# Turning the memory's keys by crossbar DMA instead of TensorE transposes

## The chip, the cores and the metric

One NeuronCore of a Trainium2 chip runs the kernel. The metric is the device time of one execution in microseconds. Inside the core, TensorE (PE, with its weight loads shown apart as PEld), VectorE (DVE), ScalarE (ACT) and GpSimd (POOL) each work through their own instructions in the order in which they were issued; SyncE (SP) issues most of the transfers. The engines wait for each other by semaphores.

## The reference

One transformer layer on 256 tokens of width 1024, in float32. What matters here is the part called cross-attention, and the piece ahead of it.

```python
def _cross_attention(h, m, w_xq, w_xkv, xq_norm_g, xk_norm_g, w_xo):
    q = (h @ w_xq).reshape(B, S, XATTN_HEADS, XATTN_HEAD_DIM)      # 4 heads of 256
    kv = (m @ w_xkv).reshape(B, M, 2, XATTN_HEADS, XATTN_HEAD_DIM) # 256 memory rows
    k, v = kv[:, :, 0], kv[:, :, 1]
    q = _rms_norm(q, xq_norm_g)
    k = _rms_norm(k, xk_norm_g)
    s = jnp.einsum('bshd,bmhd->bhsm', q, k, preferred_element_type=jnp.float32) * (XATTN_HEAD_DIM ** -0.5)
    p = jax.nn.softmax(s, axis=-1).astype(v.dtype)
    o = jnp.einsum('bhsm,bmhd->bshd', p, v).reshape(B, S, D_MODEL)
    return o @ w_xo

# in reference():
        x = x + jnp.concatenate([pool, attn], axis=-1) @ w_out[l]
        h = _rms_norm(x, norm_xattn_g[l])
        m = _rms_norm(mem, norm_mem_g[l])
        x = x + _cross_attention(h, m, w_xq[l], w_xkv[l], xq_norm_g[l], xk_norm_g[l], w_xo[l])
```

`pool` is a mixer of running means, `attn` a self-attention with 8 heads of 64. A feed-forward block with a short convolution follows.

## The kernel before, in words

**Numbers.** A float32 product is made from parts: every operand is written as a high part (fp32r, by a cast on ACT, `part_h`, L273 and L275) and a low part (the rest, by a subtraction on DVE, `part_l`, L279 and L281), and two or three PE passes add up. Weights arrive as `raw` chunks of 1 MB (two units each, a ring of three chunks), are cast to `wh` on ACT (L214) and subtracted to `wl` on DVE (L225). `need(u)` casts some units ahead of the one that PE uses; the load of a chunk can leave once the chunk that held its place in the ring has been subtracted.

**Stages, in PE's order.** The projections of the input (k, q, v, u); the memory's keys in two chunks of 512 columns, `a_chunk(18, ...)` for heads 0 and 1 and `a_chunk(22, ...)` for heads 2 and 3 (L418 to L423); between their matmuls lie the score transposes of the self-attention and the matmuls of the pool mixer; then `finish(job_attn, job_pool)`, in which the self-attention's outputs are multiplied (L651 to L655) and put into the tile `cat`; then w_out in eight output tiles (`resid_stage(26, cat, ...)`, L301 to L305), w_xq in eight, the values, w_xo, the feed-forward. `cat` has eight pieces: 0 to 3 from the pool mixer, 4 to 7 from the self-attention. Every output tile of w_out takes all eight, in the order of k.

**Order.** Work beside the matmuls is written as generators, called jobs. PE's loops call `tick()`: twice for each k of `a_chunk`, after every second k of an output tile and once more behind it (four in a tile); `finish()` ticks until its jobs are done. At a tick each live job, oldest first, goes on to its next `yield`. `yield from wait(n)` lets n ticks pass, with n from lists like `WAIT_KEY`. So the lists decide where an instruction stands in the order of its engine, and an instruction that is issued early and must wait holds up whatever its engine has behind it.

**The keys.** `key_job(c, bks)` starts when the matmuls of chunk c have been issued: `key_job(0)` just ahead of `a_chunk(22)`, `key_job(1)` just behind it. It squares the keys with a sum on ACT (L731), forms 1/rms (`head_scale`: three small DVE instructions, then twelve on POOL, L253 to L256, into `rs4y` for chunk 0 and `rs5y` for chunk 1), scales the keys out of PSUM into `kn` on DVE (L739, one half of the memory's rows at a time), turns them on PE into a bank of PSUM (L747, four 128 x 128 transposes for a head), and splits the bank into the tile `kx`.

**The cross-attention's scores.** `x_job(hp)` multiplies queries and keys of heads 2hp and 2hp+1 (L290 to L292). It is started behind query tiles 3 and 7 of w_xq, waits eight ticks, and then until the jobs named in its `after(...)` have ended.

The end of the kernel turns the residual with the crossbar already (`turn_job`, L1052 to L1060): a copy on ACT that sorts the 16-bit halves of the floats into two planes, a transposing DMA issued by SP, and copies on ACT that join the halves again.

Of the kernel before, what the change touches and what calls it, by code (L numbers as in the profile page):

```python
# [12 lines left out]
U16 = mybir.dt.uint16  # L13
# [4 lines left out]
P = 128  # L18
# [3 lines left out]
TT = S // P  # L22
# [5 lines left out]
XD = 256  # L28
# [21 lines left out]
WAIT_SCORE = [5, 4, 0, 9, 1, 6, 3, 1, 3, 5]  # L50
WAIT_ATTN = [0, 15, 1, 2, 2, 0, 0]
WAIT_POOL = [0, 8, 0, 7, 1, 5, 2, 2, 0]
WAIT_KEY = [0, 8, 7, 2, 0, 13, 5]
WAIT_R1 = [5]
WAIT_X = [3, 0, 0, 0, 10, 0, 6, 13, 8]
WAIT_VALUE = [32]
# [37 lines left out]
def block_kernel(ctx: ExitStack, tc: tile.TileContext, wpack: bass.AP, xpack: bass.AP, scal: bass.AP,  # L94
                 memT: bass.AP, table: bass.AP, out: bass.AP):
    nc = tc.nc
    pe, act, dve, pool = nc.tensor, nc.scalar, nc.vector, nc.gpsimd
# [11 lines left out]
    def bank():  # L109
        turn[0] += 1  # L110
        return psum.tile([P, 512], F32, name=f"bank{turn[0]}", tag="bank", bufs=8)

    def t2(name, dtype=F32):
        return temps.tile([P, 512], dtype, name=name, tag="t2", bufs=19)
# [4 lines left out]
    def pair(name, cols=KT * S):  # L119

        return pairs.tile([P, 2 * cols], F32R, name=name, tag="pair", bufs=4)

    def sm(name, n, dtype=F32):
        return small.tile([P, n], dtype, name=name)
# [4 lines left out]
    def go(gen):  # L129

        job = [gen, True]
        jobs.append(job)
        step(job)
        return job
# [16 lines left out]
    def wait(n):  # L151
        for _ in range(n):
            yield

    def after(*which):
        while any(job[1] for job in which):
            yield
# [5 lines left out]
    ident = tab[:, T_ID:T_ID + P]  # L163
# [95 lines left out]
    def head_scale(name, ss, n, width, small_eps):  # L259

        x = sm(name, TT * n)
        for tt in range(TT):
            c = slice(tt * n, (tt + 1) * n)
            dve.tensor_scalar(x[:, c], ss[:, c], 1.0 / width, col(small_eps, tt), op0=ALU.mult, op1=ALU.add)
        return rsqrt(x, TT * n)

    def part_h(h, src, scale=None):
        if scale is None:
            act.copy(h, src)  # L273
        else:
            act.activation(h, src, AF.Copy, scale=scale)  # L275

    def part_l(l, src, h, scale=None):
        if scale is None:
            dve.tensor_tensor(l, src, h.bitcast(F32), op=ALU.subtract)  # L279
        else:  # L280
            dve.scalar_tensor_tensor(l, src, scale, h.bitcast(F32), op0=ALU.mult, op1=ALU.subtract)  # L281
# [6 lines left out]
    def three(o, stat, mov, start, stop):  # L288

        pe.matmul(o, stat[0], mov[0], start=start, stop=False)  # L290
        pe.matmul(o, stat[0], mov[1], start=False, stop=False)  # L291
        pe.matmul(o, stat[1], mov[0], start=False, stop=stop)  # L292
# [14 lines left out]
    def col(t, c):  # L307
        return t[:, c:c + 1]

    def tiles(t, *dims):  # L310

        names = " ".join("abc"[:len(dims) - 1])
        sizes = dict(zip("abc", dims[:-1]))
        v = t.rearrange(f"p ({names} z s) -> p z {names} s", z=2, **sizes)
        return v[:, 0], v[:, 1], t.rearrange(f"p ({names} w) -> p {names} w", **sizes)
# [403 lines left out]
    kn = {}  # L719
# [3 lines left out]
    def key_job(c, bks):  # L723

        while "em" not in rows:
            yield
        yield from wait(WAIT_KEY[6])
        for mt in range(TT):
            kn[c, mt] = t2(f"kn{c}{mt}")
            for i in range(2):  # L730
                act.activation(kn[c, mt][:, i * XD:(i + 1) * XD], bks[mt][:, i * XD:(i + 1) * XD], AF.Square,  # L731
                               accum_out=col(ssk[c], 2 * mt + i))
        yield from wait(WAIT_KEY[0])
        y = head_scale(f"hm{c}", ssk[c], 2, XD, rows["em"])
        yield from wait(WAIT_KEY[1])
        for mt in range(TT):
            for i in range(2):
                r = slice(i * XD, (i + 1) * XD)
                dve.tensor_scalar(kn[c, mt][:, r], bks[mt][:, r], col(y, 2 * mt + i), None, op0=ALU.mult)  # L739
            yield from wait(WAIT_KEY[2])  # L740
        for i in range(2):
            h = 2 * c + i
            yield from wait(WAIT_KEY[3])
            b = bank()
            for dd in range(2):
                for mt in range(TT):
                    pe.transpose(b[:, (dd * 2 + mt) * P:(dd * 2 + mt + 1) * P],  # L747
                                 kn[c, mt][:, i * XD + dd * P:i * XD + (dd + 1) * P], ident)
            bb = b.rearrange("p (d s) -> p d s", d=2)
            yield from wait(WAIT_KEY[4])  # L750
            part_h(kxv[0][:, 2 * h:2 * h + 2], bb)
            yield from wait(WAIT_KEY[5])
            part_l(kxv[1][:, 2 * h:2 * h + 2], bb, kxv[0][:, 2 * h:2 * h + 2])

    for _ in range(MEM_TICKS):
# [4 lines left out]
    finish(job_k)  # L760
    kxv = tiles(pair("kx"), KT, S)
    job_key0 = go(key_job(0, bk0))
    bk1 = [bank(), bank()]
    look[0] = LOOKS[5]
    a_chunk(22, mgv, bk1)
    job_key = go(key_job(1, bk1))
    finish(job_attn, job_pool)

# [64 lines left out]
    job_r1 = []  # L833

    def x_job(hp):

        hs = (2 * hp, 2 * hp + 1)
        yield from after(job_key0, job_key, *job_r1)
        bs = [bank() for _ in range(TT)]
        for tt in range(TT):  # L840
            for i, h in enumerate(hs):
                o = bs[tt][:, i * XD:(i + 1) * XD]
                for dd in range(2):
                    q = [t[:, 2 * h + dd, tt * P:(tt + 1) * P] for t in xqv[:2]]
                    three(o, q, [t[:, 2 * h + dd] for t in kxv[:2]], dd == 0, dd == 1)
            if tt == 0:
                b = bank()
                b4 = b.rearrange("p (a s) -> p a s", a=2 * TT)
                for t in range(TT):
                    for i, h in enumerate(hs):  # L850
                        pe.transpose(b4[:, 2 * t + i], sqp[h][:, t * P:(t + 1) * P], ident)
            yield from wait(WAIT_X[0])
            if tt == 0:
                ssx = sm(f"ssx{hp}", 2 * TT)
                dve.tensor_reduce(ssx, b4, axis=AX.X, op=ALU.add)
                s2 = head_scale(f"hx{hp}", ssx, 2, XD, r1[0])
                pool.tensor_scalar(s2, s2, XD ** -0.5, None, op0=ALU.mult)
        pvs = []
        mx, nb, sums2, rec = (sm(f"{n}{hp}", 2 * TT) for n in ("xmx", "xnb", "xsum", "xrec"))
        for tt in range(TT):  # L860
            bb = bs[tt].rearrange("p (h k) -> p h k", h=2)
            c = slice(2 * tt, 2 * tt + 2)
            dve.tensor_reduce(mx[:, c], bb, axis=AX.X, op=ALU.max)
            dve.scalar_tensor_tensor(nb[:, c], mx[:, c], -1.0, s2[:, c], op0=ALU.mult, op1=ALU.mult)
            yield from wait(WAIT_X[1])
            pv = t2(f"xp{hp}{tt}").rearrange("p (h k) -> p h k", h=2)
            for j in range(2):
                cc = 2 * tt + j
                act.activation(pv[:, j], bb[:, j], AF.Exp, bias=col(nb, cc), scale=col(s2, cc),
                               accum_out=col(sums2, cc))  # L870
            pvs.append(pv)
        yield from wait(WAIT_X[2])
        for tt in range(TT):
            c = slice(2 * tt, 2 * tt + 2)
            dve.reciprocal(rec[:, c], sums2[:, c])
            for j in range(2):
                dve.tensor_scalar(pvs[tt][:, j], pvs[tt][:, j], col(rec, 2 * tt + j), None, op0=ALU.mult)
            yield from wait(WAIT_X[3])
        yield from wait(WAIT_X[4])
        if not ptv:  # L880
            ptv.extend(tiles(pair("xpt"), XH, TT, S))
        for j, h in enumerate(hs):
            b = bank()
            bb = b.rearrange("p (m q) -> p m q", m=TT)
            for mt in range(TT):
                for tt in range(TT):
                    pe.transpose(bb[:, mt, tt * P:(tt + 1) * P], pvs[tt][:, j, mt * P:(mt + 1) * P], ident)
            yield from wait(WAIT_X[5])
            part_h(ptv[0][:, h], bb)
            yield from wait(WAIT_X[6])  # L890
            part_l(ptv[1][:, h], bb, ptv[0][:, h])
        yield from wait(WAIT_X[7])
# [18 lines left out]
    for f in range(KT):  # L911
        b = bank()
# [32 lines left out]
    for h in range(XH):  # L945
        b = bank()
# [78 lines left out]
    for i in range(NFF):  # L1025
# [8 lines left out]
        for g in range(2):  # L1034
            b = bank()
# [41 lines left out]
    for c in range(2):  # L1077
        bk = [bank(), bank()]
        n = NFF - (BY_ROWS if c else 0)
# [18 lines left out]
    for tt in range(TT):  # L1098
        last = tt == TT - 1
        m = NFF - (BY_HALVES if last else 0)  # L1100
# [16 lines left out]
        b = bank()  # L1117
# [107 lines left out]
```

## Time and profile before

| | |
|---|---|
| median of 3 runs | 379.22 us (378.79 to 379.77) |
| the profiled execution | 379.3 us, span 377.3 us |
| PE | 372.6 us busy, 99% of the span |
| DVE | 314.3 us, 83% |
| ACT | 257.3 us, 68% |
| POOL | 69.5 us, 18% |

The span is the time from the first to the last instruction that the profile shows; the execution's time has 2.0 us more. Matmuls are pipelined and a PE instruction's shown duration overlaps the next ones, so what a group of them costs is read from the distance between starts. In a row of a timeline stand the start, the duration (both in us), the engine, the line of the program, the operation, the tile written and the tiles read, the shape, a count, and, in brackets, how long the engine stood idle before and what ended that.

### The profile page before, as it was taken

Reading aid. Unit: us, or ns where it says so; the run is one execution under the profiler, and the core shown is the slowest. Engines: PE = TensorE matmul, PEld = TensorE weight load, DVE = VectorE, ACT = ScalarE, POOL = GpSimd, SP = SyncE. Lnnn points to the kernel's source line nnn. Section 1 sums busy time; section 2 is a strip of 40 time slices with the busy share of each in tenths; the row PEclk is TensorE's granted clock in tenths of the full one; section 3 lists DMA queues with packets and bytes.
Section 4 is the critical chain, followed back from the end, with each engine's and each line's share of the span. In section 5 each row is a group of like instructions: output and inputs, shape, how many; then the busy total and the mean of one; then the engine's idle time right before and its main releaser. Section 6 shows DMA issues by size and latency. Waiting matters only on the chain.

```text
span 377.3 us, 5801 instructions
## 1 busy us (share of the span) xinstructions
PE 372.6 (99%) x2072; PEld 321.0 (85%) x2072; DVE 314.3 (83%) x561; ACT 257.3 (68%) x495; POOL 69.5 (18%) x151
## 2 busy tenths in 40 slices
PE   9999999999999999999999999999999999999996
PEld 7788888888888988898888888888888888888885
DVE  5699999979878969689979999999999999725611
ACT  5767887977567655855665588788777787993400
POOL 0253885143831132200320000000000000000000
PEclk9999999999999999999999999999999999999999
DMA  7996382454506535353536156655556635792501
GB/s 264 421 379 219 122 333 74 160 213 128 209 2 222 224 111 195 140 224 112 186 125 248 28 196 224 222 187 187 200 210 222 215 129 217 177 378 67 213 0 56
DMA packets 16203, 70.17 MB, mean 186 GB/s; under 512 B 5552, under 2 KB 6192, under 8 KB 8624
## 3 DMA queue, kind: packets, MB, share of 16 engines
q1 hardware_dynamic: 15888, 69.29, 51.1%
q10 hardware_dynamic: 288, 0.52, 0.4%
q8 instruction: 16, 0.26, 0.3%
q14 instruction: 11, 0.09, 0.1%
HBM read 67.71 MB, written 1.05 MB: 182 GB/s over the span
## 4 chain that ended last, share of the span: by engine, by line
PE 96%; DMA 2%; DVE 0%; ACT 0%; issue 0%; DVEq 0%
PE bank L305 33%; PE bank L304 17%; PE bank L418 7%; PE bank L423 7%; PE bank L420 7%; PE bank L1083 4%; PE bank L1088 4%; PE bank L1085 4%; DMA raw<-wpack 2%; PE bank L292 1%; PE bank L290 1%; PE bank L291 1%; PE bank L1105 1%; PE bank L1104 1%; PE bank L576 1%; PE bank L615 1%
## 5 line engine op out<-in xcount | busy, mean ns | idle before, releaser
L225 DVE TENSOR_TENSOR wl<-raw,wh 128x1024 fp32r<-128x1024 f32 (+1 forms) x127 | 150.7, 1202 | 10.5 <-ACT wh L214 10.3
L214 ACT CAST wh<-raw 128x1024 fp32r<-128x1024 f32 (+1 forms) x125 | 126.5, 1028 | 24.9 <-DMA raw<-wpack 22.6
L305 PE MATMUL bank<-hs,wh 128*128 128x512 f32 x304 | 105.4, 391 | 0.0
L304 PE MATMUL bank<-hs,wl 128*128 128x256 f32 x304 | 85.1, 280 | 0.0
L305 PEld LDWEIGHTS bank<-hs,wh 128*128 128x128 f32 x304 | 56.8, 187 | 12.5
L304 PEld LDWEIGHTS bank<-hs,wl 128*128 128x128 f32 x304 | 57.5, 189 | 0.0
L1002 ACT ACTIVATE y<-up,sc 128x256 f32<-128x256 f32 x44 | 26.2, 603 | 22.2 <-DVE up L989 17.7
L305 PE MATMUL bank<-h,wh 128*128 128x512 f32 x112 | 39.4, 394 | 0.0
L1009 DVE SCALAR_TENSOR_TENSOR y<-up,sc,y 128x255 f32<-128x255 f32 (+1 forms) x88 | 36.9, 488 | 0.0
L304 PE MATMUL bank<-h,wl 128*128 128x256 f32 x112 | 31.7, 283 | 0.0
L305 PEld LDWEIGHTS bank<-h,wh 128*128 128x128 f32 x112 | 21.0, 188 | 4.7
L1083 PE MATMUL bank<-wh,act 128*128 128x512 f32 x72 | 22.2, 389 | 0.0
L1085 PE MATMUL bank<-wh,act 128*128 128x512 f32 x72 | 22.2, 389 | 0.0
L1088 PE MATMUL bank<-wl,act 128*128 128x512 f32 x72 | 22.1, 389 | 0.0
L275 ACT ACTIVATE h<-sc 128x256 fp32r<-128x256 f32 x16 | 8.2, 511 | 20.3 <-DVE sc L793 20.2
L305 PE MATMUL bank<-cat,wh 128*128 128x512 f32 x62 | 21.8, 393 | 0.0
L305 PE MATMUL bank<-ox,wh 128*128 128x512 f32 x62 | 21.6, 394 | 0.0
L304 PEld LDWEIGHTS bank<-h,wl 128*128 128x128 f32 x112 | 21.2, 189 | 0.0
L418 PE MATMUL bank<-wh,xg 128*128 128x512 f32 x64 | 20.2, 397 | 0.5 <-ACT wh L214 0.4
L418 PE MATMUL bank<-wh,mg 128*128 128x512 f32 x64 | 20.7, 405 | 0.0
L801 POOL TENSOR_TENSOR h_acc<-h_sq,h_acc 128x256 f32<-128x256 f32 x14 | 12.9, 922 | 41.6 <-ACT h_sq L800 41.5
L423 PE MATMUL bank<-wl,mg 128*128 128x512 f32 x64 | 20.0, 394 | 0.0
(265 smaller groups left out, 733.1 us busy)
## 6 DMA issues: line engine op xcount, KB each, us to landing
raw<-wpack SPq DMA_DIRECT2D x59, 1024.0 KB, 4.9
raw<-wpack SPq DMA_DIRECT2D x4, 512.0 KB, 7.6
mraw<-memT SPq DMA_DIRECT2D x4, 256.0 KB, 8.5
sc<-xpack SPq DMA_DIRECT2D x3, 256.0 KB, 4.6
raw<-wpack ACTq DMA_DIRECT2D x2, 256.0 KB, 3.4
raw<-wpack SPq DMA_DIRECT2D x2, 256.0 KB, 4.1
out<-o SPq DMA_DIRECT2D x2, 256.0 KB, 2.6
tab<-table SPq DMA_DIRECT2D x1, 480.0 KB, 9.4
```

Source lines behind the costliest of these rows:

```text
L214: copy(split[u][0][:, r], unit(u)[:, r])
L225: dve.tensor_tensor(l[:, r], unit(u)[:, r], h[:, r].bitcast(F32), op=ALU.subtract)
L304: pe.matmul(b[:, 0:n], stat[1], mov[:, 0:n], start=start, stop=False, skip_group_check=not wide_first)
L305: pe.matmul(b, stat[0], mov, start=False, stop=stop, skip_group_check=not wide_first)
L418: pe.matmul(bk[tt], a[tt][0], wv[0], start=k == 0, stop=False)
L420: pe.matmul(bk[tt], a[tt][1], wv[0], start=False, stop=False)
L423: pe.matmul(bk[tt], a[tt][0], wv[1], start=False, stop=k == KT - 1)
L1002: act.activation(y[:, g * S:(g + 1) * S], src[:, g * S:(g + 1) * S], AF.Identity, bias=col(sc, C_CB + f), scale=col(sc, C_CW + 2 * 2 * NFF ...
L1009: dve.scalar_tensor_tensor(yy[:, j:], uu[:, :S - j], col(sc, C_CW + (2 - j) * 2 * NFF + f), yy[:, j:], op0=ALU.mult, op1=ALU.add)
L1083: pe.matmul(bk[tt], a[tt][0], w[0], start=k == 0, stop=False)
L1085: pe.matmul(bk[tt], a[tt][1], w[0], start=False, stop=False)
L1088: pe.matmul(bk[tt], a[tt][0], w[1], start=False, stop=k == NFF - 1)
```

## The change

The PE transposes of the keys go. Each half of the rows of a chunk, once scaled, is copied by ACT into two planes of 16-bit halves (`kp`), one SP queue transfer for each half transposes the planes into `kf`, and for each head ACT joins the halves into a float tile `kT` in SBUF, from which the high and low parts are made. The pauses of the key jobs are new: the squares come right after the chunk's matmuls, the scaling earlier, and chunk 1 lets 32 ticks pass between its transposes and its first join. The first cross-attention job waits for the first key job only.

```diff
-WAIT_KEY = [0, 8, 7, 2, 0, 13, 5]
+WAIT_KEY = [1, 8, 1, 0, 0, 2, 0]
+WAIT_FLAT = [[6, 1, 0, 16, 3, 6], [2, 2, 0, 32, 2, 6]]
...
         yield from wait(WAIT_KEY[0])
         y = head_scale(f"hm{c}", ssk[c], 2, XD, rows["em"])
         yield from wait(WAIT_KEY[1])
+        flat = []
         for mt in range(TT):
             for i in range(2):
                 r = slice(i * XD, (i + 1) * XD)
                 dve.tensor_scalar(kn[c, mt][:, r], bks[mt][:, r], col(y, 2 * mt + i), None, op0=ALU.mult)
-            yield from wait(WAIT_KEY[2])
+            yield from wait(WAIT_FLAT[c][mt])
+            planes = t2(f"kp{c}{mt}").bitcast(U16)
+            act.copy(planes.rearrange("p (z n) -> p z n", z=2),
+                     kn[c, mt].bitcast(U16).rearrange("p (n z) -> p z n", z=2))
+            flat.append((planes, t2(f"kf{c}{mt}").bitcast(U16)))
+            if mt == 0:
+                yield from wait(WAIT_KEY[2])
+        pauses = WAIT_FLAT[c]
+        yield from wait(pauses[2])
+        for planes, to in flat:
+            nc.sync.dma_start_transpose(to.rearrange("p (g s) -> p g s", g=8), planes)
+        yield from wait(pauses[3])
         for i in range(2):
             h = 2 * c + i
-            yield from wait(WAIT_KEY[3])
-            b = bank()
-            for dd in range(2):
-                for mt in range(TT):
-                    pe.transpose(b[:, (dd * 2 + mt) * P:(dd * 2 + mt + 1) * P],
-                                 kn[c, mt][:, i * XD + dd * P:i * XD + (dd + 1) * P], ident)
-            bb = b.rearrange("p (d s) -> p d s", d=2)
-            yield from wait(WAIT_KEY[4])
+            kT = t2(f"kT{c}{i}")
+            for mt in range(TT):
+                act.copy(kT.bitcast(U16).rearrange("p (d m s z) -> p m z d s", d=2, m=2, z=2)[:, mt],
+                         flat[mt][1].rearrange("p (z i d s) -> p i z d s", z=2, i=2, d=2)[:, i])
+                yield from wait(pauses[4])
+            bb = kT.rearrange("p (d s) -> p d s", d=2)
             part_h(kxv[0][:, 2 * h:2 * h + 2], bb)
-            yield from wait(WAIT_KEY[5])
+            yield from wait(pauses[5])
             part_l(kxv[1][:, 2 * h:2 * h + 2], bb, kxv[0][:, 2 * h:2 * h + 2])
...
-        yield from after(job_key0, job_key, *job_r1)
+        yield from after(*([job_key0] if hp == 0 else [job_key0, job_key]), *job_r1)
```

## The prediction

> **What bounds the kernel now.** I read the page's busy shares and its chain that ended last, then the timelines of PE, ACT, DVE and POOL between 69 and 106 us, where the memory's keys are made.
>
> ```profile
> PE 372.6 (99%) x2072; PEld 321.0 (85%) x2072; DVE 314.3 (83%) x561; ACT 257.3 (68%) x495; POOL 69.5 (18%) x151
> PE 96%; DMA 2%; DVE 0%; ACT 0%; issue 0%; DVEq 0%
> ```
>
> PE is busy 99% of the span, and 96% of the chain is PE. No later wait on weights stands in that chain, so a microsecond taken from PE's stream, or a hole put into it, should arrive at the end in full. ACT and DVE count only where they hold PE up.
>
> **What is removed.** Sixteen PE transposes, in four groups of four.
>
> ```profile
> L747 PE MATMUL bank<-tab,kn x16: 270/272/273, 92.5 to 115.7; 128*128 128x128 f32 x16
> ...
> 103.11 0.39 PE L305 MATMUL bank<-cat,wh 128*128 128x512 f32 x1
> 103.34 0.60 PE L747 MATMUL bank<-tab,kn 128*128 128x128 f32 x4
> ...
> 103.90 0.40 PE L305 MATMUL bank<-cat,wh 128*128 128x512 f32 x1
> ...
> 104.25 0.40 PE L305 MATMUL bank<-cat,wh 128*128 128x512 f32 x1
> ```
>
> L305 to L305 is 0.35 us without a group (103.90 to 104.25) and 0.79 with one (103.11 to 103.90): a group costs 0.44, four cost 1.77. That is the gain, 379.3 - 1.8 = 377.5 if nothing else moves. The Trainium skill (TensorE: Matmul & The Clock Gate, Part 4: PE-mode transpose) gives about 275 ns for a transpose inside a kernel; counted as PE time that would be an estimate of 4.4 us for sixteen, and the sum below would be 377.7. The trace has the same 272 ns as duration, but four overlap and take 0.44 us of the stream, so the measurement decides for 1.77.
>
> **What is added, and its prices.** The end of the kernel already turns another tensor this way.
>
> ```profile
> L1052 ACT COPY rp<-sc x4: 1030/1041/1042, 319.9 to 330.8; 128x1024 uint16<-128x1024 uint16 x4
> L1060 ACT COPY rT<-rf x8: 758/764/770, 327.8 to 342.3; 128x512 uint16<-128x512 uint16 x8
> L1056 SPq DMA_TRANSPOSE rf<-rp x4: 1237/1358/2888, 321.0 to 331.9; - x4
> DMA to landing us min/median/max: 3.1/6.1/7.4
> ```
>
> Four plane copies (4 x 1.04) and eight joins (8 x 0.76) are 10.3 us more for ACT. The casts and subtractions of the turned keys stay, from SBUF instead of PSUM; I count them as equal. SP gets four transposes of 1.2 to 2.9 us each, and they are queued between weight loads.
>
> **Where the steps fall.** A job goes on at every tick; I counted ticks from the second half of the keys' matmuls (16 ticks, two per k), tick 0 being its start. First chunk: its squares were at tick 5 and come to 0; scaling of the first half of the rows was at 13, comes to 9; its planes at 15; second half's scaling 20 to 16; its planes and both transposes at 17; joins at 33, 36, 45, 48; last subtraction at 57, as before. Second chunk: squares 21 to 16; planes 27 and 30, transposes 30; joins 62, 64, 72, 74; last subtraction 82 (was 73). The two cross-attention jobs start at 76 and 92, as before: with the relaxed condition the first does not wait for 82, and the second comes after it. So PE's order is unchanged but for the missing transposes.
>
> The trouble is at tick 20. There the attention's four outputs, cat tiles 4 to 7, are cast on ACT, and PE needs them at once, in the first output tile of w_out. Before, nothing of the keys stood ahead of them on ACT. Now the first planes (15), the second chunk's squares (16) and the second planes (17) do.
>
> ```profile
> 69.84 2.02 ACT L214 CAST wh<-raw 128x1024 fp32r<-128x1024 f32 x2
> 71.73 0.59 ACT L605 ACTIVATE p<-bank,nbs,sp 128x256 f32<-128x256 f32 x1
> ...
> 72.73 0.23 ACT L605 ACTIVATION_READ_ACCUMULATOR p<-bank,nbs,sp 128x1 f32 x1
> ...
> 75.37 0.43 ACT L731 ACTIVATE kn<-bank 128x256 f32<-128x256 f32 x1
> ...
> 76.81 0.44 ACT L624 COPY pt<-bank 128x256 f32<-128x256 f32 x1
> ...
> 81.44 0.47 ACT L275 ACTIVATE cat<-bank,sc 128x256 fp32r<-128x256 f32 x1 [0.55 <-DVE cat L281]
> ...
> 82.33 0.50 ACT L275 ACTIVATE cat<-bank,sc 128x256 fp32r<-128x256 f32 x1
> 84.24 0.47 ACT L275 ACTIVATE cat<-bank,sc 128x256 fp32r<-128x256 f32 x1 [1.42 <-DVE cat L281]
> 84.61 0.67 ACT L273 CAST cat<-bank 128x256 fp32r<-128x256 f32 x2
> ...
> 86.22 0.37 ACT L273 CAST cat<-bank 128x256 fp32r<-128x256 f32 x1 [0.28 <-PE bank L655]
> ```
>
> ```profile
> 73.81 0.16 DVE L607 RECIPROCAL recs<-sums 128x2 f32<-128x2 f32 x1
> ...
> 74.53 0.16 DVE L607 RECIPROCAL recs<-sums 128x2 f32<-128x2 f32 x1
> ...
> 77.28 0.17 DVE L246 TENSOR_SCALAR rs4y<-hm 128x4 int32<-128x4 int32 x1
> 77.36 0.69 DVE L701 TENSOR_TENSOR pooll<-pf,poolh 128x512 fp32r<-128x512 f32 x1
> 77.96 2.35 DVE L225 TENSOR_TENSOR wl<-raw,wh 128x1024 fp32r<-128x1024 f32 x2
> ...
> 82.94 0.88 DVE L739 TENSOR_SCALAR kn<-bank,rs4y 128x256 f32<-128x256 f32 x2 [0.51 <-POOL rs4y L256]
> 83.73 0.48 DVE L281 SCALAR_TENSOR_TENSOR cat<-bank,sc,cat 128x256 fp32r<-128x256 f32 x1
> ...
> 86.63 0.42 DVE L279 TENSOR_TENSOR cat<-bank,cat 128x256 fp32r<-128x256 f32 x1 [0.23 <-ACT cat L273]
> ```
>
> ```profile
> 77.53 0.57 POOL L253 TENSOR_TENSOR rs4t<-rs4y 128x4 f32<-128x4 f32 x1 [10.11 <-DVE rs4y L246]
> 78.18 1.06 POOL L254 TENSOR_TENSOR rs4t<-rs4t,hm 128x4 f32<-128x4 f32 x1
> 79.33 1.04 POOL L255 TENSOR_SCALAR rs4t<-rs4t 128x4 f32<-128x4 f32 x1
> ...
> 82.70 0.20 POOL L256 TENSOR_TENSOR rs4y<-rs4t,rs4y 128x4 f32<-128x4 f32 x1
> ```
>
> ```profile
> 87.61 0.28 PE L304 MATMUL bank<-cat,wl 128*128 128x256 f32 x1
> 87.73 0.40 PE L305 MATMUL bank<-cat,wh 128*128 128x512 f32 x1
> ...
> 88.79 0.40 PE L305 MATMUL bank<-cat,wh 128*128 128x512 f32 x1
> ```
>
> Before, the last cat tile was done on DVE at 87.05 (86.63 + 0.42), and PE's k=7 reads it at 88.79: a margin of 1.74 us. Now the same chain after the change.
>
> 1. The squares move ahead of the two weight casts at 69.84 and push what follows by 1.44 (75.37 to 76.81), so the softmax piece of 71.73 runs at 73.17 and its sums are read by 74.4 (1.23 later, as 71.73 to 72.96). DVE, in order, normalizes it (0.72, 73.81 to 74.53) and only then forms the variances and rs4y (three of 0.17 at most, about 0.4): 75.55, and POOL's twelve steps start 0.25 later (77.28 to 77.53), at 75.8 instead of 77.53.
> 2. Three of POOL's steps before took 0.6 to 1.06 us and ended with DVE's pooll and wl instructions (78.05, 79.1, 80.3); the other nine took 0.28 each (to 82.90). DVE has a softmax scaling, three such instructions up to 79.2, so five steps by then and seven at 0.28: rs4y at 81.3.
> 3. The scaling of the keys (0.85) now stands on DVE ahead of a wl (1.15) and of the pool mixer's cat subtractions (0.48); before it stood behind two of them. First subtraction done at 83.8. ACT's next cat cast waits for it (the 0.55 and 1.42 waits): 83.85; third cast 0.89 later (81.44 to 82.33), its subtraction 0.50 later, the fourth cast 0.51 after that (83.73 to 84.24): 85.75.
> 4. Behind it (0.37): planes 0.95, squares 1.44, planes 0.95 (1.04 copies follow each other in 0.95, as the casts of 1.04 do). The four cat casts start at 89.45 instead of 84.61.
> 5. From first cast to last subtraction 2.1 (four times 0.42, and 0.41 ahead): 91.55. PE wanted it at 88.79, so PE stands **2.75 us**, most of it before k=4.
>
> **The other edits.** Two places where I count nothing.
>
> ```profile
> 89.03 3.85 SPq L186 DMA_DIRECT2D raw<-wpack  x2
> sum 15.00, PE 15.00 PEld 13.34 DVE 13.13 ACT 11.97 POOL 2.24; mean PE 5.00 PEld 4.45 DVE 4.38 ACT 3.99 POOL 0.75
> 124.86 0.97 DVE L281 SCALAR_TENSOR_TENSOR xq<-xq,ggx,xq 128x256 fp32r<-128x256 f32 x1
> 127.30 0.28 PE L290 MATMUL bank<-kx,xq 128*128 128x256 f32 x1
> ```
>
> SP: the first two transposes wait for their planes until about 89.4 and take 2 x 1.36 to issue, so the weight load behind them, at 89.03 before, leaves at about 92.2. Its weights are used in the ninth tile from there, the first of w_xq (8 x 2.8 us on, a tile being 8 x 0.35); cost nothing, and without that cover up to the 3.2 us. The second chunk's transposes come at tick 30, behind the loads asked for earlier; the load after them belongs to w_xq's third tile. The first join comes 16 ticks (0.7 us each, 11 us) after the issue, against 2.7 to issue and at most 7.4 to land.
>
> ACT in w_xq: from 115 to 130 us (the windows' sum) it is busy 11.97 of 15, and four joins bring 3.06: full to the brim. PE is covered by weights cast two tiles ahead (5.6 us), and by 1.5 us at the closest place: the subtraction of query tile 3 was done at 125.8, the first scores came at 127.30. I take 0; the bounds are 0 and the 1.5 us by which 3 us of lateness would pass that cover.
>
> Below nothing is excluded for both. DVE's work in w_out is the same but starts later; its idle stretches there take that up.
>
> **Sum.** -1.77 + 2.75 + 0 = +1.0 on the profiled execution's 379.3 (span 377.3 and 2.0 around it), which stands 0.1 above the median of 379.22; on the median it gives 380.2. A difference of 0.3% (1.14 us) is about what a measurement here can tell from none: the lines are 378.08 and 380.36.
>
> **The rivals.**
> - *The hole in PE does not open (faster).* With no POOL step held up, rs4y is there at 75.8 + 12 x 0.28 = 79.2, DVE never waits, and the cat casts start at 87.35: a hole of 0.65, 378.1. If ACT's plane copies overlap better, none: 377.5. For it: ACT idled 2.25 us in the rows shown of that stretch (0.55, 1.42, 0.28). Against: 3.34 us are put in front, more than the 1.74 of margin, and POOL's slow steps stand in the rows. Chance 0.28.
> - *POOL's chain is as late as before (slower).* rs4y at 82.9 because more DVE instructions fall into its steps; it decides from 81.5 on, where the hole passes 2.9 us. At 82.9 the hole is 4.3 and the time 381.8. For it: DVE is busy through all the first five steps; against: the start is 1.7 us earlier. Chance 0.07.
> - *PE's clock falls in the hole (slower).* If the stop before k=4 reaches 3.8 us (4.3 less the last tiles' part) and the remaining four pairs of 0.35 run at half speed, that adds 1.4: 383.2. The Trainium skill (TensorE: Matmul & The Clock Gate, Why this matters for your kernels) warns of idle gaps of over about 3 us, after which the clock goes back to K=4/8; no run here shows such a gap. By the forecast the stop before k=4 is 2.2 us (first cast done at 89.82, PE there at 87.61). Chance 0.03.
> - *ACT is late in w_xq (slower).* The joins cost PE 1.0 or more there, on top: 381.2. For it the full windows, against it the lead of two tiles. Chance 0.08.
>
> **How the numbers follow.** The forecast, a hole of 2 to 3.5 us, has 0.54: 379.4 to 381.0, with 380.2 in the middle; six tenths of it lie below 380.36. Faster: the first rival less its top edge, 0.25. Same: 0.33 and that edge, 0.36. Slower: 0.21 and the three others, 0.39. The range goes from 377.4 (no hole) to 381.9 (POOL late); the forecast alone would have 379.4 to 381.0.
>
> **What would show it.** L747 is gone, and the pairs of L304 and L305 run through at 0.35 where the groups stood. The cat casts L273 start near 89.5, behind a plane copy; L739's first scaling waits for POOL and ends near 82.2; PE's L304 of the first w_out tile waits for ACT's cat, with about 2.2 us before k=4. If the four casts start by 87, the third and fourth steps of my chain are wrong; if they start late and PE still runs through, my reading of what k=4 to 7 needs is wrong. If PE waits in w_xq instead, the price of the joins is what I missed.

## The result and the profile after

The changed kernel takes 383.81 us (383.16 to 385.25 in four runs) against 379.24 (378.79 to 379.77): a ratio of 1.0118, interval 1.01 to 1.0135. It is slower by 4.6 us; the forecast was +1.0. The profiled execution took 383.16 us, span 381.3 (before 379.3 and 377.3); it is the shortest of the four, so the profile accounts for 3.9 of the 4.6 us. In the changed kernel lines up to L733 have moved by one and later ones by eleven: L304 and L305 are L305 and L306, L855 is L866, L887 is L898.

The page's busy shares, and the engines' shares of the chain that ended last, after:

```profile
PE 373.3 (98%) x2056; PEld 319.5 (84%) x2056; DVE 314.0 (82%) x561; ACT 266.1 (70%) x507; POOL 71.0 (19%) x151
PE 78%; ACT 8%; DVE 6%; POOL 3%; issue 2%; DMA 1%; DVEq 0%; POOLq 0%; ACTq 0%
```

Sixteen PE instructions fewer, as told; ACT is 8.8 us busier. PE's share of the chain fell from 96% to 78%: ACT, DVE and POOL now stand in it, so PE waits for work. Where it does is seen in PE's timeline, first after, then the same places before (127.30 and 88.79 are in the prediction).

```profile
87.91 0.39 PE L306 MATMUL bank<-cat,wh 128*128 128x512 f32 x1
89.72 0.38 PE L305 MATMUL bank<-cat,wl 128*128 128x256 f32 x1 [1.42 <-ACT cat L274]
...
91.34 0.40 PE L306 MATMUL bank<-cat,wh 128*128 128x512 f32 x1
...
128.52 0.28 PE L291 MATMUL bank<-kx,xq 128*128 128x256 f32 x1
...
142.98 0.30 PE L898 MATMUL bank<-tab,xp 128*128 128x128 f32 x1
143.98 0.55 PE L898 MATMUL bank<-tab,xp 128*128 128x128 f32 x3 [0.70 <-DVE xp L888]
144.28 0.36 PE L291 MATMUL bank<-kx,xq 128*128 128x256 f32 x1
...
160.76 0.55 PE L898 MATMUL bank<-tab,xp 128*128 128x128 f32 x3 [0.76 <-DVE xp L888]
...
167.09 0.28 PE L291 MATMUL bank<-xpt,vx 128*128 128x256 f32 x1
```

```profile
141.69 0.60 PE L887 MATMUL bank<-tab,xp 128*128 128x128 f32 x4
142.04 0.36 PE L290 MATMUL bank<-kx,xq 128*128 128x256 f32 x1
...
156.85 0.63 PE L887 MATMUL bank<-tab,xp 128*128 128x128 f32 x4
...
163.27 0.28 PE L290 MATMUL bank<-xpt,vx 128*128 128x256 f32 x1
```

Three holes. In w_out's first tile PE stands before k=4; at k=7 it is 2.55 us late (91.34 against 88.79). At the first pair's scores, with all key transposes behind it, 1.22 (128.52 against 127.30): the missing transposes gave back 1.33. Then come two holes that the prediction did not have, both at the transposes of the cross-attention's softmax (L898, tile `xp`): 2.24 behind the first (144.28 against 142.04), 3.82 behind the second (167.09 against 163.27), and so to the end, where the spans differ by 4.0.

These three places, the first pair's scores (**A**), the scores behind the first softmax's transposes (**B**) and the first value product, behind the second's (**C**), serve as landmarks below. The offset is the start after less 127.30, 142.04 or 163.27. The column "start" has the offset of PE's first matmul on the memory's rows (52.27 us before), where nothing of the edits stands yet: executions differ there by up to 1.1 us, and an edit's own share is the difference to it. The order of PE's work at A or B is another in e11_wait and e12_pool_both, so they have no row.

| kernel | start | A | B | C | span, less 377.3 |
|---|---|---|---|---|---|
| after | -0.21 | +1.22 | +2.24 | +3.82 | +4.0 |
| e1_cat | -0.17 | -1.19 | +1.27 | +2.86 | +3.2 |
| e2_joins | -0.15 | +1.28 | +2.08 | +3.66 | +3.8 |
| e3_both | -0.02 | -1.01 | +1.01 | +2.60 | +2.9 |
| e7_joins_only | +0.24 | +0.24 | +0.61 | +2.22 | +2.2 |
| e8_dma_only | +0.86 | +0.86 | +0.86 | +0.84 | +1.0 |
| e4_half | -0.16 | -1.05 | -1.05 | -0.55 | -0.6 |
| e10_half_late | +0.09 | -0.80 | -0.80 | -0.94 | -0.9 |
| e14_late_only | +0.08 | +0.08 | +0.08 | -0.05 | 0.0 |
| e5_late | +0.16 | -0.86 | +3.65 | +6.72 | +6.8 |
| e6_pool | +0.07 | -0.69 | -0.23 | +1.37 | +1.5 |
| e9_pool_late | -0.16 | -1.13 | -0.37 | -0.10 | +0.8 |
| e13_first_half | -0.05 | -0.01 | -0.02 | -0.16 | +0.3 |

What holds the softmax up is seen on DVE, after and then before, and on ACT after.

```profile
81.20 0.88 DVE L741 TENSOR_SCALAR kn<-bank,rs4y 128x256 f32<-128x256 f32 x2 [2.07 <-POOL rs4y L257]
...
89.70 1.42 DVE L280 TENSOR_TENSOR cat<-bank,cat 128x256 fp32r<-128x256 f32 x4 [0.77 <-ACT cat L274]
...
132.01 0.42 DVE L908 TENSOR_TENSOR xq<-bank,xq 128x256 f32<-128x256 f32 x1 [1.24 <-ACT xq L907]
...
134.38 0.68 DVE L866 TENSOR_REDUCE ssx<-bank 128x4 f32<-128x512 f32 x1
...
140.84 0.16 DVE L875 SCALAR_TENSOR_TENSOR xnb<-xmx,rs7y 128x2 f32<-128x2 f32 x1 [2.06 <-POOL rs7y L868]
```

```profile
130.79 0.68 DVE L855 TENSOR_REDUCE ssx<-bank 128x4 f32<-128x512 f32 x1
...
136.99 0.16 DVE L864 SCALAR_TENSOR_TENSOR xnb<-xmx,rs7y 128x2 f32<-128x2 f32 x1 [0.38 <-POOL rs7y L857]
...
156.52 0.62 DVE L877 TENSOR_SCALAR xp<-xp,xrec 128x256 f32<-128x256 f32 x2
```

```profile
85.95 1.04 ACT L744 COPY kp<-kn 128x1024 uint16<-128x1024 uint16 x1
88.33 1.07 ACT L744 COPY kp<-kn 128x1024 uint16<-128x1024 uint16 x1
89.26 1.23 ACT L274 CAST cat<-bank 128x256 fp32r<-128x256 f32 x4
...
130.97 0.78 ACT L758 COPY kT<-kf 128x512 uint16<-128x512 uint16 x1
...
141.04 0.56 ACT L880 ACTIVATE xp<-bank,xnb,rs7y 128x256 f32<-128x256 f32 x1 [3.20 <-DVE xnb L875]
```

The softmax begins with sums of squares (`ssx`, DVE), goes through twelve small POOL steps and one that scales to `rs7y`, back to DVE (`xnb`), to ACT for the exponentials, to DVE for the division (`xp`), and only then to PE. `ssx` stands in DVE's order behind the addition of a query tile (L908), which waits for ACT's copy of that tile (L907). ACT has a join (L758) in front of it: the addition stood idle for 1.24 us, `ssx` started at 134.38 instead of 130.79, `xnb` 3.85 us late (140.84 against 136.99). PE itself was 1.22 late at the scores, so 2.6 of that is more than PE's own lateness.

### The profile page after: what moved, and what is told of

Same layout as the page of the kernel before. It is cut to its first block, busy times and chain, and to the rows that moved or that the text cites. A ratio compares the mean times of both kernels' runs of the same rounds, so it can differ in the third digit from the quotient of the medians.

```text
span 381.3 us, 5792 instructions
## 1 busy us (share of the span) xinstructions
PE 373.3 (98%) x2056; PEld 319.5 (84%) x2056; DVE 314.0 (82%) x561; ACT 266.1 (70%) x507; POOL 71.0 (19%) x151
## 3 DMA queue, kind: packets, MB, share of 16 engines
HBM read 67.71 MB, written 1.05 MB: 180 GB/s over the span
## 4 chain that ended last, share of the span: by engine, by line
PE 78%; ACT 8%; DVE 6%; POOL 3%; issue 2%; DMA 1%; DVEq 0%; POOLq 0%; ACTq 0%
PE bank L306 29%; PE bank L305 15%; PE bank L419 5%; PE bank L421 5%; PE bank L424 5%; PE bank L1099 4%; PE bank L1094 4%; PE bank L1096 4%; DVE wl L226 3%; ACT wh L215 1%; ACT xp L880 1%; PE bank L1116 1%; PE bank L1115 1%; DMA sc<-xpack 1%; ACT p L606 1%
## 5 line engine op out<-in xcount | busy, mean ns | idle before, releaser
L306 PE MATMUL bank<-hs,wh 128*128 128x512 f32 x304 | 105.4, 391 | 0.0
L305 PE MATMUL bank<-hs,wl 128*128 128x256 f32 x304 | 85.1, 280 | 0.0
L306 PEld LDWEIGHTS bank<-hs,wh 128*128 128x128 f32 x304 | 56.8, 187 | 12.5
L305 PEld LDWEIGHTS bank<-hs,wl 128*128 128x128 f32 x304 | 57.5, 189 | 0.0
L306 PE MATMUL bank<-h,wh 128*128 128x512 f32 x112 | 39.5, 395 | 0.0
L305 PE MATMUL bank<-h,wl 128*128 128x256 f32 x112 | 31.7, 283 | 0.0
L306 PEld LDWEIGHTS bank<-h,wh 128*128 128x128 f32 x112 | 21.0, 188 | 4.7
L306 PE MATMUL bank<-cat,wh 128*128 128x512 f32 x62 | 22.1, 400 | 0.1
L306 PE MATMUL bank<-ox,wh 128*128 128x512 f32 x62 | 21.6, 394 | 0.0
L305 PEld LDWEIGHTS bank<-h,wl 128*128 128x128 f32 x112 | 21.2, 189 | 0.0
L424 PE MATMUL bank<-wl,xg 128*128 128x512 f32 x64 | 19.9, 393 | 0.0
```

Source lines behind the costliest of these rows:

```text
L305: pe.matmul(b[:, 0:n], stat[1], mov[:, 0:n], start=start, stop=False, skip_group_check=not wide_first)
L306: pe.matmul(b, stat[0], mov, start=False, stop=stop, skip_group_check=not wide_first)
L424: pe.matmul(bk[tt], a[tt][0], wv[1], start=False, stop=k == KT - 1)
```

## The experiments

**Theory A**, formed here: two pieces of ACT's added work cost. Planes and squares ahead of the cat casts make the first hole; the second chunk's joins in w_xq delay the first softmax's sums, and PE waits at the transposes of both softmaxes. **Rival B**: the transfers, or SP's queue, cost wherever the joins stand. Comparisons give the median, and its ratio to the kernel before in the same session (379.13 to 379.40 us).

**e1_cat: the keys' ACT work behind the cat casts.**

```diff
-WAIT_KEY = [1, 8, 1, 0, 0, 2, 0]
-WAIT_FLAT = [[6, 1, 0, 16, 3, 6], [2, 2, 0, 32, 2, 6]]
+WAIT_KEY = [[0, 8, 0, 0, 0, 2, 5], [0, 8, 0, 0, 0, 2, 5]]     # one list for each chunk
+WAIT_FLAT = [[8, 1, 0, 16, 3, 6], [2, 2, 0, 29, 2, 6]]
```

> Chunk 0's planes and chunk 1's squares go behind the cat casts (squares at ticks 5 and 21, planes at 21, 22, 31, 33); joins of chunk 1 stay in w_xq. Theory A (three holes in PE, all made by ACT work that stands in front: 2.65 us at the first w_out tile, 1.2 at each of the two softmax turns of the cross-attention): the first hole goes, the two others stay, 383.8 - 2.65 = 381.2. Rival B (the transposing transfers on SP and the DMA engines are what slows it): nothing changes, 383.8, since the same four transfers run in the same stretch.

382.33 us, ratio 1.008 (1.0065 to 1.0095): 1.1 us short of what theory A expected. The first hole is gone, and PE is 1.19 us early at A; by B all of that is lost and 1.27 more. PE's timeline, and its windows with the granted clock in the column behind the busy time:

```profile
111.16 0.38 PE L305 MATMUL bank<-h,wl 128*128 128x256 f32 x1 [0.34 <-ACT h L276]
...
142.01 0.30 PE L898 MATMUL bank<-tab,xp 128*128 128x128 f32 x1 [1.37 <-DVE xp L888]
143.01 0.55 PE L898 MATMUL bank<-tab,xp 128*128 128x128 f32 x3 [0.70 <-DVE xp L888]
```

```profile
140.60:143.00 2.40, 0.34 (x2) 1.00 0.00 0
143.00:148.00 5.00, 4.99 (x25) 0.66 0.00 0
```

The first of these rows is a hole that theory A did not name: at k=7 of w_xq's first tile PE waits for ACT's `h`, and falls from 1.56 us early (the matmuls ahead) to 0.56; e13_first_half below shows why. `ssx` started at 133.42, one microsecond earlier than after, though PE was 2.4 us earlier: the softmax is set by ACT and DVE, not by PE. And the longer stop had a second price: the clock is 0.66 in the mean of the five microseconds behind it, which is half speed for 3.4 of them, 1.7 us lost.

**e2_joins and e3_both: the second chunk's joins later in w_xq**, ticks 76 to 81 instead of 62 to 76, with the rest as after (e2) or as in e1_cat (e3).

```diff
-WAIT_FLAT = [[6, 1, 0, 16, 3, 6], [2, 2, 0, 32, 2, 6]]
+WAIT_FLAT = [[6, 1, 0, 16, 3, 6], [2, 2, 0, 46, 1, 1]]     # e2_joins
+WAIT_FLAT = [[8, 1, 0, 16, 3, 6], [2, 2, 0, 43, 1, 1]]     # e3_both
```

> Only chunk 1's four joins and two casts are moved, from ticks 62 to 76 to ticks 76 to 81, where ACT waited for the first softmax. Theory A: the first hole of 2.65 us stays, the two softmax holes go, 383.8 - 2.4 = 381.4; the first softmax sum on DVE then starts about 1.2 us later than before the change, not 3.6. Rival B: 383.8. Rival C (the softmax holes come from PE being late by the first hole, not from the joins): 383.8 too, with the holes at the two turns still there.

> Both moves together. Theory A: no hole, and the sixteen PE transposes saved: 379.24 less 1.3 to 1.8, so 377.4 to 377.9. Rival B: not below 381. If a hole is left at the softmax turns because ACT has four joins more there, about 378.5.

e2_joins: ratio 1.0111 (1.0087 to 1.0135), as after. e3_both: 382.41 us, 1.0084 (1.0067 to 1.0101), as e1_cat. Both missed. DVE in e3_both tells why:

```profile
132.40 0.69 DVE L280 TENSOR_TENSOR kx<-kT,kx 128x512 fp32r<-128x512 f32 x1 [1.77 <-ACT kx L274]
133.01 0.68 DVE L866 TENSOR_REDUCE ssx<-bank 128x4 f32<-128x512 f32 x1
```

The subtraction of the turned keys, issued at tick 79 too but by the older job, now stood right ahead of `ssx` and waited 1.77 us for ACT. Later was still in front.

**e7_joins_only: the kernel before, plus four copies of a join's shape on ACT in w_xq** at the joins' ticks, whose results nobody reads. **e8_dma_only: the kernel before, plus only the four transposing transfers**, also unread.

```diff
+    def extra_job():                                          # e7_joins_only
+        yield from wait(42)
+        for i in range(2):
+            kT = t2(f"kT{i}")
+            for mt in range(TT):
+                act.copy(kT.bitcast(U16)..., kn[1, mt].bitcast(U16)...)
+                yield from wait(2)
+            yield from wait(6)
```

```diff
+        for mt in range(TT):                                  # e8_dma_only
+            nc.sync.dma_start_transpose(t2(f"kf{c}{mt}").bitcast(U16)..., kn[c, mt].bitcast(U16))
```

> The kernel before, turning keys on PE, with four added copies on ACT of the joins' size at the ticks of the changed kernel's (62, 64, 72, 74), whose results nobody reads; no planes, no transfers. Theory A: these alone delay the softmax sums, with holes at the softmax transposes of 1 to 2.4 us together: 381.2 us (380.2 to 381.8). Rival B: 379.2, no change.

> The kernel before, turning keys on PE, with the four transposing transfers added (straight from the scaled keys, 2 at tick 27 and 2 at tick 43 counted from the start of w_out's predecessor), whose results nobody reads; no planes, no joins. Theory A: 379.2 us, no change within 0.3%. Rival B: 380.2 or more, with weights or casts late in w_out.

e7_joins_only: 381.72 us, ratio 1.0068 (1.0053 to 1.0083). Its group of copies, its `ssx` and its second softmax's transposes:

```profile
L773 ACT COPY kT<-kn 128x512 uint16<-128x512 uint16 x4 | 3.1, 773 | 0.0
```

```profile
133.06 0.68 DVE L867 TENSOR_REDUCE ssx<-bank 128x4 f32<-128x512 f32 x1
```

```profile
159.14 0.55 PE L899 MATMUL bank<-tab,xp 128*128 128x128 f32 x3 [0.77 <-DVE xp L889]
```

3.1 us of ACT work and nothing else move `ssx` from 130.79 to 133.06 and PE from +0.24 at A to +2.22 at C. Less its start, e7_joins_only is 1.98 us late at C. Theory A's mechanism is shown for the joins; the 0.6 us by which the changed kernel loses more between A and C were not taken apart.

e8_dma_only: 380.23 us, ratio 1.0012 (0.9998 to 1.0027). The profiled execution is 0.86 late at A, but it is so from the first weights on, where nothing of the edit stands yet: an early wait of PE for weights, in e8_dma_only and then before.

```profile
11.52 0.73 PE L418 MATMUL bank<-wh,xg 128*128 128x512 f32 x2 [0.80 <-ACT wh L214]
```

```profile
10.66 0.74 PE L418 MATMUL bank<-wh,xg 128*128 128x512 f32 x2 [0.45 <-ACT wh L214]
```

From there 0.86 stays 0.86 at A and at B, 0.84 at C. Rival B falls: the transfers cost nothing that the landmarks show. They leave SP at 93.8 to 102 us here, later than in the changed kernel (87.0 to 100.1); but there too the profile shows no wait of PE for weights between 60 and 180 us, only waits for `cat` and `xp`. One thing stays open: of the ten executions of e8_dma_only four took 378.99 to 379.27 us and six 380.17 to 380.59, and only one of the six was profiled. The whole lateness of that one is there from the start; what makes the five others late, and why six of ten are, no run shows.

**e4_half: the kernel before without half of the transposes.** Heads 1 and 3 take the turned keys of heads 0 and 2, so half of the keys' turning is left out. **e10_half_late**: the same, and the second softmax's transposes stand three ticks later in PE's order. **e14_late_only**: the kernel before with only that delay.

```diff
-            b = bank()
-            for dd in range(2):
+            b = bank() if i == 0 else b
+            for dd in range(2 if i == 0 else 0):
...
-        yield from wait(WAIT_X[4])
+        yield from wait(WAIT_X[4] + (0, 3)[hp])               # e10_half_late, e14_late_only
```

> The kernel before with 8 of the 16 transposes of the keys left out (heads 1 and 3 take the turned keys of heads 0 and 2), nothing put in their place. It measures the gain by itself. Theory A with 0.44 us for four: 379.24 - 0.88 = 378.4. With 272 ns of PE for each: 379.24 - 2.2 = 377.1. If the softmax chain of the cross-attention sets the end there already: no change.

> e4_half (the kernel before without 8 of its 16 key transposes, heads 1 and 3 taking heads 0 and 2's turned keys) with the second softmax's transposes 3 ticks later. Theory A: the 0.89 us won by the transposes is kept to the end instead of 0.3 to 0.5: 378.3 us (377.9 to 378.6). Rival (part of the gain is lost elsewhere): 378.8 as e4_half.

> The kernel before with only the second softmax's transposes 3 ticks later. Theory A: PE did not wait there, so nothing is won: 379.2 us, same within 0.3%. Rival (the later place is what makes e10_half_late fast): 378.7 or less.

e4_half: 378.83 us, ratio 0.9987 (0.9978 to 0.9996). PE started 0.16 ahead and is 1.05 ahead at A and B: 0.89 for eight transposes, twice the prediction's 0.44. Then it has to wait:

```profile
155.80 0.27 PE L887 MATMUL bank<-tab,xp 128*128 128x128 f32 x1
156.40 0.55 PE L887 MATMUL bank<-tab,xp 128*128 128x128 f32 x3 [0.33 <-DVE xp L877]
```

The division that these transposes read ended at 157.14 before (156.52 + 0.62), just behind PE's arrival at 156.85: the margin was none, and a PE that comes earlier stands there. With the transposes later, e10_half_late keeps all of it: 378.28 us, 0.9976 (0.9967 to 0.9985), -0.94 at C (of the 1.03 from its start, the later place alone makes 0.13, as e14_late_only shows). By itself the delay wins nothing: e14_late_only 379.21 us, 0.9999 (0.9991 to 1.0008).

**e5_late: the second chunk's joins behind the first softmax**, the rest as in e1_cat.

```diff
-WAIT_FLAT = [[8, 1, 0, 16, 3, 6], [2, 2, 0, 29, 2, 6]]
+WAIT_FLAT = [[8, 1, 0, 16, 3, 6], [2, 2, 0, 50, 1, 1]]
```

> The keys' work as in e1_cat (behind the cat casts), but the four joins of the second chunk and the casts and subtractions that follow them stand behind the first softmax (from tick 83 on, ahead of the second pair's scores at tick 92). Theory A (the key work that stands on ACT and DVE ahead of the first softmax's sums delays that softmax, and PE waits for it): the sums start at about 130.8 as in the kernel before, the 2.07 us hole at the first softmax's transposes is gone, PE comes there some 1.2 us early; the second softmax had no margin and now has 2.8 us of joins and subtractions near it, so part is given back there. 379.2 us, 378.5 to 380.2. Rival B (the transposing transfers or the queue that issues them cost, wherever the joins are): stays at 382.

385.92 us, ratio 1.0175 (1.016 to 1.019): the sum missed, one step right. DVE's and PE's timelines, and PE's windows:

```profile
130.72 0.68 DVE L866 TENSOR_REDUCE ssx<-bank 128x4 f32<-128x512 f32 x1
```

```profile
145.69 0.58 PE L291 MATMUL bank<-kx,xq 128*128 128x256 f32 x1 [4.27 <-ACT kx L274]
```

```profile
141.00:145.00 4.00, 0.41 (x4) 0.91 0.00 0
145.00:151.00 6.00, 4.97 (x18) 0.50 0.76 268
151.00:153.00 2.00, 2.00 (x10) 0.97 0.59 250
```

Without joins in front `ssx` is back at 130.72. But PE wants the second chunk's keys right behind the first softmax's transposes, and they were not split yet: a 4.27 us hole, and half speed for about 6.8 us. So on ACT neither of the places that were tried is free, before the first softmax or behind it.

**e6_pool: the second chunk's joins on POOL**, the rest as in e1_cat. **e9_pool_late** adds the three ticks before the second softmax's transposes, **e12_pool_both** two ticks before the first's as well.

```diff
-                act.copy(kT.bitcast(U16)...
+                (act.copy if c == 0 else pool.tensor_copy)(kT.bitcast(U16)...
```

> As e1_cat with the same ticks, but the second chunk's four joins are copied by POOL instead of ACT. Theory A: ACT's work in w_xq is as long as before, the first softmax's sums start within 1 us of the kernel before, 379.6 us (378.8 to 380.5), as long as POOL's copies are done before its own steps in the softmax chain; where they are not, it is over 382 and rs7y is late. Rival B: 382.3 as e1_cat.

> e6_pool with the second softmax's eight transposes 3 ticks (about 3 us of PE work) later in PE's order; nothing else moved. Theory A (the second softmax's chain over DVE and POOL stood level with PE in the kernel before, so whatever PE wins ahead of it is waited away there): the 1.1 to 1.4 us hole at the second softmax's transposes goes, PE stays 0 to 0.2 us behind the kernel before at the end: 379.3 us (378.6 to 380.0). Rival (the chain's lateness passes on to what follows the transposes, heads 2 and 3 of the value products): no change from e6_pool, 380.8.

> e9_pool_late with the first softmax's transposes 2 ticks later as well. Theory A: the 0.5 us or so of hole there goes too: 378.9 us (378.1 to 379.8). Rival, as for e9_pool_late: 380.8.

e6_pool: 380.77 us, ratio 1.0041 (1.0026 to 1.0056), 1.6 less than e1_cat. e9_pool_late: 380.44, 1.003 (1.0019 to 1.0042). e12_pool_both: 380.61, 1.0037 (1.0025 to 1.0049). In e6_pool POOL takes 4.5 us for the four, and `ssx` comes at 132.04: still 1.25 late. ACT and DVE keep the planes, the first chunk's joins and the splitting; which of them it is was not taken apart. In e9_pool_late the second softmax's hole is gone (-0.10 at C), but the lateness goes on into the value products, +0.71 behind them (the first w_xo matmul at 169.73 against 169.02), where PE waits for `vx` among others. In e12_pool_both no wait is left at the transposes, but PE waits 0.68 us for ACT's `xq` at the second pair's scores (142.41) and again for `vx`. Theory A was half right here: moving PE's reader moves the wait.

**e11_wait: the changed kernel with the first pair waiting for all keys again.**

```diff
-        yield from after(*([job_key0] if hp == 0 else [job_key0, job_key]), *job_r1)
+        yield from after(job_key0, job_key, *job_r1)
```

> The changed kernel with the first pair's job waiting for all keys again, as the kernel before had it; the first softmax starts 6 ticks later and its transposes stand 6 ticks later in PE's order, the second pair's job stays where it is. Theory A: the chain of the first softmax has no joins in its way any more and the hole at its transposes goes; w_out's hole and the second softmax's stay: 381.5 to 382.6 us. Rival (the earlier start of the first pair is what keeps the softmax hidden): a hole of some us at the first pair's transposes, over 385.

387.84 us, ratio 1.0234 (1.0215 to 1.0254): the rival's side. The last keys come at tick 82, so both softmaxes stand close together, and the second is late:

```profile
162.77 0.30 PE L898 MATMUL bank<-tab,xp 128*128 128x128 f32 x1 [2.54 <-DVE xp L888]
```

Part of it is clock: 0.65 in the mean of the 4.8 us behind that stop. But not all of the difference belongs to the condition. In this execution the clock fell behind w_out's stop too, long before the first pair's job, at a stop as long as in the changed kernel (1.42 us in both, 89.72 there):

```profile
89.83 0.38 PE L305 MATMUL bank<-cat,wl 128*128 128x256 f32 x1 [1.42 <-ACT cat L274]
```

```profile
84.00:91.50 7.50, 5.56 (x55) 1.00 0.31 59
91.50:94.91 3.41, 3.41 (x12) 0.50 0.63 146
94.91:98.00 3.09, 3.09 (x19) 1.00 1.02 342
```

Ahead of the first pair's scores PE is therefore 2.29 us late, against 1.22 in the changed kernel: 1.1 of the 4.3 us between the two profiled spans are not the edit's. Given the late joins, the relaxed condition is worth about 3 us in these two executions; it is a part of the change that pays.

**e13_first_half: only the first chunk by DMA**, at e1_cat's places, the second on PE as before, with e10_half_late's delay.

```diff
-WAIT_KEY = [1, 8, 1, 0, 0, 2, 0]
+WAIT_KEY = [[0, 8, 0, 0, 0, 2, 5], [0, 8, 7, 2, 0, 13, 5]]   # by chunk
...
+        if c == 1:
+            ...  # pe.transpose, part_h and part_l as in the kernel before
+            return
```

> Only the first chunk (heads 0 and 1) is turned by DMA, with its planes and squares behind the cat casts and its joins on ACT at the ticks of e1_cat; the second chunk is turned on PE as in the kernel before. The second softmax's transposes stand 3 ticks later in PE's order, as in e10_half_late. Theory A (what costs is ACT's work in front of the cat casts and in w_xq; both are gone here, but for the last of the first chunk's joins at the start of w_xq): 0.89 us won by eight transposes less, 0.3 to 0.5 given back at h1's first tile, none at the softmaxes: 378.8 us (378.4 to 379.6). Rival (any join on ACT from w_out's end on comes out at the softmaxes): 379.8 or more.

379.62 us, ratio 1.001 (1.0001 to 1.0019): not faster, and just between theory A's range and the rival's. PE is 0.96 early at the end of w_out and 0.13 late behind k=7 of w_xq's first tile, so all of the gain is spent there. PE's row, then DVE's, and DVE's before:

```profile
111.84 0.38 PE L305 MATMUL bank<-h,wl 128*128 128x256 f32 x1 [0.42 <-ACT h L276]
```

```profile
109.77 0.69 DVE L280 TENSOR_TENSOR kx<-kT,kx 128x512 fp32r<-128x512 f32 x1
110.37 0.88 DVE L822 TENSOR_TENSOR sc<-bank,sc 128x256 f32<-128x256 f32 x2
```

```profile
110.00 0.88 DVE L793 TENSOR_TENSOR sc<-bank,sc 128x256 f32<-128x256 f32 x2 [0.27 <-PE bank L305]
```

The subtraction of the turned keys stands on DVE right ahead of w_out's last additions (`sc`), from which ACT makes the `h` of k=7; before, those additions waited for PE alone. A stop of 0.42 us in the row costs 1.1 us of PE's offset. Another 0.4 goes among the value products (the first w_xo matmul at 169.36 against 169.02, from 0.16 early at C). No kernel here that does all of the work beats the one before; e10_half_late does, by leaving half of the turning out.

## Why the prediction was wrong

**The gain, -1.77.** The price of a group was right (0.89 for two in e4_half). In the changed kernel 1.33 of 1.77 arrived at A. Most of the rest lies in the pitch of the pairs: in w_out from 92 to 112 us the starts of L306 are 0.353 us apart, 0.347 before, which is 0.3 to 0.4 us over some 57 pairs. Why, no run settles. And the gain could not have reached the end whole: the second softmax had no margin. The statement that a microsecond taken from PE's stream arrives in full rested on a chain that was 96% PE; such a chain does not show how close behind it the next one runs.

**The hole, +2.75.** Right in its steps and its size. `rs4y` came at 81.17 (forecast 81.3), the cat casts started at 89.26 (89.45), behind a plane copy, and PE, 0.21 early in the stages ahead, left k=7 2.55 late: 2.76, of which 0.7 stood already ahead of the tile's first matmul (86.63 against 86.10). The two rivals about this hole, none and POOL late, did not occur; in the profiled execution the clock stayed at full speed here. The last of POOL's twelve steps:

```profile
80.97 0.20 POOL L257 TENSOR_TENSOR rs4y<-rs4t,rs4y 128x4 f32<-128x4 f32 x1
```

**SP, 0.** Right in the cost: PE waited for no weights, and e8_dma_only adds nothing that the landmarks show. The load behind the first transposes left at 92.28 (forecast about 92.2), but that this agrees is in part luck: the transposes were through by 90.66, and the load then waited 1.6 us for DVE's subtraction of the chunk in its place.

```profile
87.02 3.64 SPq L752 DMA_TRANSPOSE kf<-kp  x2
92.28 3.39 SPq L187 DMA_DIRECT2D raw<-wpack  x2
```

**ACT in w_xq, 0: the step that failed.** 2.6 us from A to C, 2.0 with the joins alone in e7_joins_only. The cover named was the weights' lead of two tiles and the 1.5 us of a query tile, and it held: PE did not wait in w_xq. The work behind was overlooked. The additions of the query tiles, which wait for ACT, share DVE's order with `ssx`, whose chain over POOL, DVE and ACT had 1.35 us of margin at the first softmax (`xp` done at 139.72 + 0.62, PE there at 141.69) and none at the second. The section on the kernel before says that an instruction that must wait holds up whatever its engine has behind it; I looked as far as PE's next reader and not at the two jobs that start at ticks 76 and 92. The bound of 1.5 us was too small for the same reason, and the rival "ACT is late in w_xq" (0.08, +1.0) had the right cause, the wrong place and less than half of the size.

**The clock.** The rival put it in w_out's hole. In the profiled execution of the changed kernel it did not fall there, and in that of e11_wait, with the same stop of 1.42 us, it did; so that it stayed up was in part luck, and the rival's condition, a stop of 3.8 us, was too strict. At the first softmax it fell in e1_cat (four executions with a mean granted clock of 0.994 or 0.995). The longest of the changed kernel's four, 385.25 us, has a mean of 0.994 too; where it fell there is not on record.

Put together: -1.33 and +2.76 and +2.6 make the 4.0 us of the spans.

## What to carry over

Work that is added to an engine with idle time is free only where nothing that waits behind it is due: follow each engine's order on to the next long chain (here DVE, POOL, DVE, ACT, DVE, PE for a softmax) and read its margin, not only that of PE's next operand. An 0.44 us group of transposes on a pipelined PE is cheap beside the 2.6 us of copies on ACT that replace it. When PE is 99% busy, ask how far behind it the second chain is before counting a saving in full.

## What the runs showed of the hardware

A stop shorter than expected can halve the clock, and its length alone does not decide. In e1_cat PE stood for 2.06 of 2.40 us, with only transposes between, and then ran at half speed for 3.4 us; in e5_late it was 6.8 us after a stop of 4.27. In e3_both 1.64 of the same 2.40 us (busy 0.76) cost no clock. In e11_wait the stop of 1.42 us in w_out was followed by 3.41 us at half speed (91.50 to 94.91), and the same stop in the changed kernel and in e2_joins by none. The two half-speed stretches of e11_wait begin at 91.50 and 163.18 us, 21 times 3.41 us apart. What decides in a single case no run settles. The Trainium skill (TensorE: Matmul & The Clock Gate, Part 1, What's actually happening) has a free-running window of about 3.4 us over which activity is judged; the lengths of the half-speed stretches, one and two such windows, agree. Its advice in Why this matters for your kernels, no idle gap over about 3 us, is not enough here: 2.06 us was too much in e1_cat and 1.42 us in e11_wait, and the measurement decides.

Joins take 0.77 us on ACT and 1.18 us on POOL (mean of four in e6_pool). The pitch of an L305 and L306 pair is either 0.347 or 0.353 us and stays so for stretches of ten microseconds and more, in the kernel before too (0.353 from 116 to 128 us).
